# Position transform of the Fourier branch: plain fp32 products in place of split ones

## The chip, the core and the metric

The kernel runs on one core of a Trainium2 chip. Its engines work side by side, each on its own queue: TensorE (PE in the profile; its weight loads are a row of their own, PEld) multiplies matrices, VectorE (DVE) and ScalarE (ACT) work on elements, GpSimd (POOL) does little here, and SyncE's queue (SP) issues the DMAs. The metric is the time of one execution on the device in microseconds (us), the median of several runs. Before the change it is 1631.18 us (3 runs, 1630.85 to 1631.53).

## What is computed

Two layers of an encoder on 256 positions with 1024 channels. Each has a mixer of three branches (window attention, a state-space scan, a Fourier mixing) behind one input projection, then a cross-attention into 256 memory tokens, then a gated feed-forward. The change touches the Fourier branch only: six groups of 256 channels, of each the real part of the two-dimensional DFT over positions and channels.

```python
f = f_in.reshape(bsz, seq, FOURIER_GROUPS, FOURIER_GROUP_DIM).astype(f32)
f = jnp.fft.fft2(f, axes=(1, 3), norm="ortho").real.astype(h.dtype).reshape(bsz, seq, FOURIER_WIDTH)
y_fourier = f @ w_b_fourier
```

## The kernel before

**Split products.** Large products are made of three products in a reduced fp32 format (F32R): a value is split into a high part, its F32R rounding, and a low part, the rest. `mm3` (lines 352 to 355) adds high x high, high x low and low x high in PSUM. The weights come as a stream of 1 MB pieces on SP's queue (`load_next`, L313); each piece is split by an ACT cast (L323) and a DVE subtraction (L324) into `wh` and `wl`, up to three pieces ahead. `lin` (products with 512 columns, lines 353 to 355) and `lina` (256 columns, lines 414 to 416) run the projections over them. Attention and scan use plain fp32 products (`T.matmul` on fp32 tiles: L603, L648, L848, L849).

**The Fourier branch.** The input projection is taken in the order of `ORDER`; its first three tokens in each layer are f0, f1 and f2, and then bc, k0, x0 and the rest. One f token gives 512 columns, two channel groups. `lin` yields them for the positions 0 to 127 (`tt` = 0) and 128 to 255 (`tt` = 1). `f_done` folds the two halves, since cosine and sine over 256 positions are symmetric: sum and difference of the halves. It copies the first half out of PSUM on ACT (L1086), adds and subtracts on DVE (L1088, L1089), and splits both results, each with an ACT cast (L1091) and a DVE subtraction (L1092).

`fourier_chunk` then runs in two stages. The first is the position transform: for each group `j`, half `ct` of its channels and parity `e`, a product of 128 channels (stationary) with a 128x128 table of cosines and sines (moving, 128 columns) into `pg`, by `mm3`. Then ACT copies one half (L919), DVE forms sums and differences `uv` (L920, L921), ACT and DVE split them (L923, L924). The second stage is the channel transform with 264 and 256 columns, again by `mm3`, then the evacuation (L942 to L952). The table `c_dft` has six 128x128 blocks: two for the first stage, four for the second. `dft_parts` loads it in each layer (L895) and splits all six (L897, L898).

**What sets the order.** `lin` and `lina` write the main sequence. Other work is written as generators in four lanes (`n`, `s`, `a`, `f`); Fourier work is in lane `f`. After each half piece `pump` adds credit and lets the lanes take steps, and a step charges what it yields (`yield 0.9`). `yield 3, 0` means that the step wants three free 4 KB slots and no 2 KB slot; `slot` forces steps when slots become few. `yield LATER` holds the lane back for some pumps. A scheduler at compile time then orders the instructions of each engine; inside `ordered()` TensorE's own order is kept as written. On the chip each queue runs in order.

Of the kernel before, what the change touches and what calls it, by code (L numbers as in the profile page):

```python
# [11 lines left out]
F32 = mybir.dt.float32  # L12
F32R = mybir.dt.float32r
# [4 lines left out]
P = 128  # L18
# [153 lines left out]
def trunk(ctx: ExitStack, tc: tile.TileContext, a, out):  # L172
    nc = tc.nc
    V, A, T, G = nc.vector, nc.scalar, nc.tensor, nc.gpsimd
# [19 lines left out]
    def slot(size, shape, dt):  # L194
        keep = 0 if running[0] else RESERVE
        while len(slots[size]) <= keep and step():
            pass
        if not slots[size]:
            raise RuntimeError(f"no slot of {size} KB")
        r = slots[size].popleft()  # L200
        t = r.tile(shape, dt, name=nm("s%d_" % size))
        owner[id(t)] = (size, r, t)
        return t

    def s4(shape, dt=F32):
        return slot(4, shape, dt)

    def s2(shape, dt=F32):
        return slot(2, shape, dt)

    def free(*ts):
        for t in ts:
            if isinstance(t, (tuple, list)):
                free(*t)
            else:
                size, r, _ = owner.pop(id(t))
                slots[size].append(r)
# [25 lines left out]
    def bg(gen, lane="s"):  # L243
        lanes[lane].append(gen)
# [103 lines left out]
    def ordered():  # L348

        return tc.manual_schedule(engines={mybir.EngineType.PE})  # L350

    def mm3(o, sh, sl, mh, ml, start, stop):
        T.matmul(o, sh, mh, start=start, stop=False)  # L353
        T.matmul(o, sh, ml, start=False, stop=False)  # L354
        T.matmul(o, sl, mh, start=False, stop=stop)  # L355
# [66 lines left out]
    def fl(tiles):  # L422
        return lambda kt: tiles[kt // 4]
# [54 lines left out]
    def norms(n):  # L478

        drain_until(lambda: len(lanes["n"]) <= n, "n")  # L480
# [14 lines left out]
    def ftiles(n):  # L495
        return [(s4([P, 4, S], F32R), s4([P, 4, S], F32R)) for _ in range(n)]
# [263 lines left out]
    def bc_fin(bc, idx):  # L760

        def fin(v):
            hi, lo = bc
            A.copy(hi[:, idx:idx + 2, :], v)
            V.tensor_sub(lo[:, idx:idx + 2, :], v, hi[:, idx:idx + 2, :].bitcast(F32))
            yield 0.6
        return fin
# [122 lines left out]


    def dft_parts(R):
        yield 3, 0
        r = s4([P, 6, P])
        nc.sync.dma_start(r, a["c_dft"])  # L895
        hi, lo = R["dft"] = s4([P, 6, P], F32R), s4([P, 6, P], F32R)
        A.copy(hi, r)  # L897
        V.tensor_sub(lo, r, hi.bitcast(F32))  # L898
        free(r)
        yield 0.9  # L900

    def fourier_chunk(l, c, f, FT, R):


        yield 2, 0

        Gt = (s4([P, 2, 2, S], F32R), s4([P, 2, 2, S], F32R))
        dh, dl = R["dft"]
        for j in range(2):
            yield 0, 2  # L910
            pg = tp().rearrange("p (a b) -> p a b", a=2)
            with ordered():
                for ct in range(2):
                    cs = slice((2 * j + ct) * P, (2 * j + ct + 1) * P)
                    for e in range(2):
                        mm3(pg[:, ct, e * P:e * P + P], f[0][:, e, cs], f[1][:, e, cs], dh[:, e, :], dl[:, e, :],
                            True, True)
            t0, uv = s2([P, S]), s2([P, 2, S])
            A.copy(t0, pg[:, 0, :])  # L919
            V.tensor_add(uv[:, 0, :], t0, pg[:, 1, :])  # L920
            V.tensor_sub(uv[:, 1, :], t0, pg[:, 1, :])  # L921
            hi, lo = (t[:, :, j, :] for t in Gt)
            A.copy(hi, uv)  # L923
            V.tensor_sub(lo, uv, hi.bitcast(F32))  # L924
            free(t0, uv)
            yield 1.3
        free(f)
        yield LATER
        yield 2, 0
        out_ = FT[c] = (s4([P, 4, S], F32R), s4([P, 4, S], F32R))  # L930
        gp = [t.rearrange("p u j (b k) -> p u (j b) k", b=2) for t in Gt]
        for cp_ in range(2):

            qc, qs = (t[:, :4 * n].rearrange("p (j k) -> p j k", j=4) for t, n in ((tp(), 66), (tp(), 64)))
            with ordered():
                for m, o, k0, k1 in ((2, qc, 0, 66), (4, qs, 64, 128)):
                    m += cp_
                    mm3(o, dh[:, m, :], dl[:, m, :], gp[0][:, cp_, :, k0:k1], gp[1][:, cp_, :, k0:k1], True, True)
            yield 0, 2
            pc = s2([P, 4, 66])  # L940
            fo = s2([P, 2, S])
            A.copy(pc, qc)  # L942
            p4 = pc.rearrange("p (j b) k -> p j b k", j=2)
            q4 = qs.rearrange("p (j b) k -> p j b k", j=2)

            V.tensor_sub(fo[:, :, 0:P].rearrange("p j (m b) -> p j b m", b=2), p4[:, :, :, 0:64], q4)
            V.tensor_add(fo[:, :, P + 2:S:2], p4[:, :, 0, 63:0:-1], q4[:, :, 0, 63:0:-1])
            V.tensor_add(fo[:, :, P + 1:S:2], p4[:, :, 1, 63::-1], q4[:, :, 1, ::-1])
            A.copy(fo[:, :, 0:S:P], p4[:, :, 0, 0:65:64])
            hi, lo = (t.rearrange("p (j e) k -> p j e k", e=2)[:, :, cp_, :] for t in out_)  # L950
            A.copy(hi, fo)
            V.tensor_sub(lo, fo, hi.bitcast(F32))  # L952
            free(pc, fo)
            yield 1.8
        free(Gt)
        if R.get("f") == 2:
            free(R["dft"])
        R["f"] = R.get("f", 0) + 1
# [30 lines left out]
    for l in range(L):  # L989
# [10 lines left out]
        def to_T(kind, g):  # L1000
            t = s4([P, 2, 512])
            qkv[kind, g] = t

            def f(tt, ch, ps):
                A.copy(t[:, tt, :], ps)
            return f

        R = {}
# [58 lines left out]
        def xbc_pieces(blk, fin_of):  # L1067
            def f(n0, ps):
                pair = (n0 - X0) // 256 - blk // 2
                bg(conv_pair(ps, blk + 2 * pair, cw, fin_of(pair)))  # L1070
            lina(hb, 2, f)
# [3 lines left out]
        for n, tok in enumerate(ORDER):  # L1075
            k, g = tok[0], int(tok[1]) if tok[1].isdigit() else 0
            sg = [2] if n == 0 else None
            if k == "f":
                ft = (s4([P, 2, 512], F32R), s4([P, 2, 512], F32R))

                fs = []

                def f_done(tt, ch, ps, ft=ft, fs=fs):
                    if tt == 0:
                        fs.extend((s2([P, 512]), s2([P, 512])))
                        A.copy(fs[0], ps)  # L1086
                        return
                    V.tensor_add(fs[1], fs[0], ps)  # L1088
                    V.tensor_sub(fs[0], fs[0], ps)  # L1089
                    for e, t in enumerate(fs[::-1]):  # L1090
                        A.copy(ft[0][:, e, :], t)  # L1091
                        V.tensor_sub(ft[1][:, e, :], t, ft[0][:, e, :].bitcast(F32))  # L1092
                    free(fs)

                lin(hb, 2, f_done, seg=sg, mid=sg and (lambda: norms(0)))
                bg(fourier_chunk(l, g, ft, FT, R), "f")
            elif tok == "bc":
                dt_columns()
                Bt, Ct = ftiles(2)
                xbc_pieces(16, lambda pr: bc_fin(Bt, 2 * pr))  # L1100
                xbc_pieces(20, lambda pr: bc_fin(Ct, 2 * pr))
                bg(cb_task(l, Bt, Ct, R))
            elif k == "x":
                xT = s4([P, 2, 512])
                xbc_pieces(4 * g, lambda pr: x_fin([xT], pr))
                bg(ssd_group(l, g, xT, R, Dbc, ys))
            elif k in "qkv":
                lin(hb, 2, to_T(k, g), seg=sg, par=True)
                if k == "v":
                    bg(attn_group(l, g, qkv["q", g], qkv["k", g], qkv["v", g], gq[:, 2:3], R), "a")  # L1110
            elif k == "z":
                zt = s4([P, 2, 512])
                lin(hb, 2, lambda tt, ch, ps, zt=zt: A.activation(zt[:, tt, :], ps, AF.Silu))
                bg(ssd_gate(l, g, zt, ys, yT))
            elif k == "G":
                ga = gates(g)
            elif tok == "BF":
                drain_until(lambda: R.get("f") == 3, "f")
                branch(fl(FT), 8, ga)
                free(*FT.values(), ga)  # L1120
            elif tok == "BA":
                drain_until(lambda: "oT" in R and R.get("a"), "a")
                branch(fl(R["oT"]), 2, ga)
                free(R["oT"], ga)
# [304 lines left out]
```

## Time and profile before

| | |
|---|---|
| median of 3 runs | 1631.18 us (1630.85 to 1631.53) |
| profiled execution | 1631.55 us, its span 1629.8 us |
| TensorE busy | 1611.2 us, 99% of the span, 10354 products |
| DVE busy | 1164.7 us, 71% |
| ACT busy | 974.2 us, 60% |
| POOL busy | 45.9 us, 3% |
| granted TensorE clock | full, in all 40 slices |
| weights and data from HBM | 293.65 MB, 181 GB/s over the span |
| chain that ended last | PE 94%, ACT 3%, DVE 2%, issue 1% |

The span is the time between the first and the last instruction of the profiled execution; the 1.75 us beyond it lie around it. A product's end in the trace is modelled and overlaps the next product, so a busy TensorE row is not TensorE at its peak: the distance from one start to the next tells what a product costs in the queue. A wait is put down to the event that came last.

### The profile page before, as it was taken

The page shows a single profiled execution, that of the slowest core. Times are in us where ns is not written, and L with a number is a line of the kernel's source. Part 1 is how long each engine was busy: PE and PEld are TensorE (multiplying, and loading weights), DVE is VectorE, ACT ScalarE, POOL GpSimd, SP SyncE. Part 2 cuts the span into 40 slices and gives each one's busy share as a digit, 9 for nine tenths or more (in the row PEclk, how much of TensorE's full clock was granted, in tenths as well). Part 3 has the DMA queues.
Part 4 walks back from the last instruction along what each step waited for, and adds up shares of the span by engine and source line. Part 5 has one row for each costly group of instructions (what it writes and reads, how often), then busy time and mean ns, then how long its engine had stood idle before and what let it go on. Part 6 is the DMA issues. An engine that isn't in the chain of part 4 may idle for free.

```text
span 1629.8 us, 25584 instructions
## 1 busy us (share of the span) xinstructions
PE 1611.2 (99%) x10354; PEld 1454.3 (89%) x10354; DVE 1164.7 (71%) x1803; ACT 974.2 (60%) x1639; POOL 45.9 (3%) x47
## 2 busy tenths in 40 slices
PE   7999999999999999999999999999999999999998
PEld 6899988898998888999879998888989988889997
DVE  6898878788966665555479988868888676665543
ACT  6566667778745665444355667677786357554441
POOL 0000000000100100000000000000000001000000
PEclk9999999999999999999999999999999999999999
DMA  8445754656556544555553567555455555445552
GB/s 280 152 153 188 237 202 149 203 172 178 194 177 228 178 156 156 206 181 192 181 170 123 175 213 226 195 170 180 168 187 194 182 206 181 143 158 179 183 189 93
DMA packets 84302, 296.52 MB, mean 182 GB/s; under 512 B 7529, under 2 KB 46825, under 8 KB 53976
## 3 DMA queue, kind: packets, MB, share of 16 engines
q1 hardware_dynamic: 84184, 294.89, 54.0%
q8 instruction: 81, 1.33, 0.3%
q14 instruction: 37, 0.30, 0.1%
HBM read 293.65 MB, written 1.22 MB: 181 GB/s over the span
## 4 chain that ended last, share of the span: by engine, by line
PE 94%; ACT 3%; DVE 2%; issue 1%; POOL 0%; DMA 0%; SPq 0%; DVEq 0%; ACTq 0%; POOLq 0%
PE acc L354 14%; PE acc L355 14%; PE acc L353 14%; PE acc L415 13%; PE acc L414 13%; PE acc L416 13%; PE tp L848 2%; ACT wh L323 2%; PE tp L353 1%; PE tp L355 1%; PE tp L354 1%; PE tp L849 1%; PE tp L473 1%; PE tp L648 1%; PE tp L603 1%; DVE wl L324 1%
## 5 line engine op out<-in xcount | busy, mean ns | idle before, releaser
L324 DVE TENSOR_TENSOR wl<-wr,wh 128x2048 fp32r<-128x2048 f32 (+2 forms) x260 | 573.3, 2207 | 283.9 <-ACT wh L323 283.3
L323 ACT CAST wh<-wr 128x2048 fp32r<-128x2048 f32 (+2 forms) x260 | 477.4, 1839 | 402.2 <-issue 181.2
L414 PE MATMUL acc<-s,wh 128*128 128x256 f32 x1856 | 527.9, 285 | 0.0
L415 PE MATMUL acc<-s,wh 128*128 128x256 f32 x1856 | 526.6, 284 | 0.0
L416 PE MATMUL acc<-s,wl 128*128 128x256 f32 x1856 | 525.5, 283 | 0.0
L353 PE MATMUL acc<-wh,s 128*128 128x512 f32 x1072 | 427.7, 399 | 0.0
L354 PE MATMUL acc<-wl,s 128*128 128x512 f32 x1072 | 424.4, 396 | 0.4 <-DVE wl L324 0.4
L355 PE MATMUL acc<-wh,s 128*128 128x512 f32 x1072 | 423.7, 396 | 0.0
L415 PEld LDWEIGHTS acc<-s,wh 128*128 128x128 f32 x1856 | 356.1, 192 | 1.3 <-issue 0.5
L414 PEld LDWEIGHTS acc<-s,wh 128*128 128x128 f32 x1856 | 355.8, 192 | 1.6 <-issue 0.9
L416 PEld LDWEIGHTS acc<-s,wl 128*128 128x128 f32 x1856 | 355.8, 192 | 0.0
L355 PEld LDWEIGHTS acc<-wh,s 128*128 128x128 f32 x1072 | 203.6, 190 | 41.6 <-issue 1.4
L353 PEld LDWEIGHTS acc<-wh,s 128*128 128x128 f32 x1072 | 203.9, 190 | 41.2 <-issue 1.9
L354 PEld LDWEIGHTS acc<-wl,s 128*128 128x128 f32 x1072 | 203.8, 190 | 41.0 <-issue 0.9
L689 DVE SCALAR_TENSOR_TENSOR s<-s,cw,s 128x253 f32<-128x253 f32 (+2 forms) x288 | 121.7, 476 | 1.1 <-ACT s L686 0.7
L820 ACT ACTIVATE s<-s,nacs 128x128 f32<-128x128 f32 x128 | 44.6, 394 | 15.2 <-DMA s<-dd 13.9
L823 ACT ACTIVATE s<-s,dt 128x128 f32<-128x128 f32 x128 | 43.8, 395 | 2.7 <-DVE s L604 2.1
L821 DVE SCALAR_TENSOR_TENSOR s<-s,nacs,s 128x128 f32<-128x128 f32 x128 | 41.5, 344 | 5.0 <-ACT s L820 5.0
L353 PE MATMUL tp<-s,s 128*128 128x256 f32 (+2 forms) x152 | 42.8, 284 | 1.7 <-ACT s L923 1.5
L355 PE MATMUL tp<-s,s 128*128 128x256 f32 (+2 forms) x152 | 42.6, 283 | 0.5 <-DVE s L1092 0.5
L354 PE MATMUL tp<-s,s 128*128 128x256 f32 (+2 forms) x152 | 42.4, 280 | 0.0
L489 DVE TENSOR_TENSOR s<-tp,s 128x512 fp32r<-128x512 f32 x56 | 36.6, 683 | 5.6 <-ACT s L488 5.6
(223 smaller groups left out, 1419.7 us busy)
## 6 DMA issues: line engine op xcount, KB each, us to landing
wr<-in_wstream SPq DMA_DIRECT2D x236, 1024.0 KB, 4.9
s<-dd SPq DMA_DIRECT2D x32, 512.0 KB, 5.3
wr<-in_wstream SPq DMA_DIRECT2D x16, 768.0 KB, 4.4
s<-vd SPq DMA_DIRECT2D x12, 256.0 KB, 6.1
wr<-in_wstream SPq DMA_DIRECT2D x8, 256.0 KB, 4.7
s<-in_ssd_norm_g SPq DMA_DIRECT2D x8, 256.0 KB, 5.4
s<-in_memT SPq DMA_DIRECT2D x4, 512.0 KB, 5.9
X<-in_x SPq DMA_DIRECT2D x2, 512.0 KB, 3.8
```

The costliest lines, as they stand in the source:

```text
L323: A.copy(hi[:, c], raw[:, c])
L324: V.tensor_sub(lo[:, c], raw[:, c], hi[:, c].bitcast(F32))
L353: T.matmul(o, sh, mh, start=start, stop=False)
L354: T.matmul(o, sh, ml, start=False, stop=False)
L355: T.matmul(o, sl, mh, start=False, stop=stop)
L414: T.matmul(o, hi[:, w0:w0 + P], sh[:, k, :], start=kt == 0, stop=False)
L415: T.matmul(o, hi[:, w0:w0 + P], sl[:, k, :], start=False, stop=False)
L416: T.matmul(o, lo[:, w0:w0 + P], sh[:, k, :], start=False, stop=kt == npk - 1)
L689: V.scalar_tensor_tensor(v[:, b, i0:i1], u[:, b, i0 + k - 3:i1 + k - 3], c[:, k:k + 1], v[:, b, i0:i1], op0=ALU.mult, op1=ALU.add)
L820: A.activation(E[:, j, :], b[:, 1, :], AF.Identity, bias=nacs[:, tt, 32 + hf:33 + hf])
L821: V.scalar_tensor_tensor(E[:, j, :], b[:, 0, :], nacs[:, tt, hf:hf + 1], E[:, j, :], op0=ALU.add, op1=ALU.min)
L823: A.activation(W[:, j, :], cbd[:, tt, 0, :], AF.Copy, scale=dt[:, tt, hf:hf + 1])
```

## The change

`dft_parts` loads the two blocks of the first stage into a plain fp32 tile `dt_` (a 2 KB slot) and the four of the second into a scratch tile; only these four are split, into the two halves of one 4 KB tile `hl`. `f_done` writes sum and difference into one plain fp32 tile of the chunk and no longer splits them; the copy of the first half goes into the same tile. The first stage of `fourier_chunk` multiplies the two plain tiles with one fp32 product in place of `mm3`. The second stage reads the same four blocks from `hl`. The credit charged for the constants is 0.7 in place of 0.9, and the step wants two 4 KB slots and one 2 KB slot in place of three 4 KB slots.

```diff
--- before.py
+++ after.py
@@ -890,14 +890,17 @@
 
 
     def dft_parts(R):
-        yield 3, 0
-        r = s4([P, 6, P])
-        nc.sync.dma_start(r, a["c_dft"])
-        hi, lo = R["dft"] = s4([P, 6, P], F32R), s4([P, 6, P], F32R)
-        A.copy(hi, r)
-        V.tensor_sub(lo, r, hi.bitcast(F32))
+        yield 2, 1
+
+        dt_, r = s2([P, 2, P]), s4([P, 4, P])
+        nc.sync.dma_start(dt_, a["c_dft"][:, 0:2])
+        nc.sync.dma_start(r, a["c_dft"][:, 2:6])
+        hl = s4([P, 2, 4, P], F32R)
+        A.copy(hl[:, 0], r)
+        V.tensor_sub(hl[:, 1], r, hl[:, 0].bitcast(F32))
         free(r)
-        yield 0.9
+        R["dft"] = dt_, hl
+        yield 0.7
 
     def fourier_chunk(l, c, f, FT, R):
 
@@ -905,7 +908,7 @@
         yield 2, 0
 
         Gt = (s4([P, 2, 2, S], F32R), s4([P, 2, 2, S], F32R))
-        dh, dl = R["dft"]
+        dt_, hl = R["dft"]
         for j in range(2):
             yield 0, 2
             pg = tp().rearrange("p (a b) -> p a b", a=2)
@@ -913,8 +916,7 @@
                 for ct in range(2):
                     cs = slice((2 * j + ct) * P, (2 * j + ct + 1) * P)
                     for e in range(2):
-                        mm3(pg[:, ct, e * P:e * P + P], f[0][:, e, cs], f[1][:, e, cs], dh[:, e, :], dl[:, e, :],
-                            True, True)
+                        T.matmul(pg[:, ct, e * P:e * P + P], f[:, e, cs], dt_[:, e, :], start=True, stop=True)
             t0, uv = s2([P, S]), s2([P, 2, S])
             A.copy(t0, pg[:, 0, :])
             V.tensor_add(uv[:, 0, :], t0, pg[:, 1, :])
@@ -933,9 +935,9 @@
 
             qc, qs = (t[:, :4 * n].rearrange("p (j k) -> p j k", j=4) for t, n in ((tp(), 66), (tp(), 64)))
             with ordered():
-                for m, o, k0, k1 in ((2, qc, 0, 66), (4, qs, 64, 128)):
+                for m, o, k0, k1 in ((0, qc, 0, 66), (2, qs, 64, 128)):
                     m += cp_
-                    mm3(o, dh[:, m, :], dl[:, m, :], gp[0][:, cp_, :, k0:k1], gp[1][:, cp_, :, k0:k1], True, True)
+                    mm3(o, hl[:, 0, m, :], hl[:, 1, m, :], gp[0][:, cp_, :, k0:k1], gp[1][:, cp_, :, k0:k1], True, True)
             yield 0, 2
             pc = s2([P, 4, 66])
             fo = s2([P, 2, S])
@@ -1076,21 +1078,15 @@
             k, g = tok[0], int(tok[1]) if tok[1].isdigit() else 0
             sg = [2] if n == 0 else None
             if k == "f":
-                ft = (s4([P, 2, 512], F32R), s4([P, 2, 512], F32R))
-
-                fs = []
-
-                def f_done(tt, ch, ps, ft=ft, fs=fs):
+                ft = s4([P, 2, 512])
+
+                def f_done(tt, ch, ps, ft=ft):
+                    u, v = ft[:, 0, :], ft[:, 1, :]
                     if tt == 0:
-                        fs.extend((s2([P, 512]), s2([P, 512])))
-                        A.copy(fs[0], ps)
+                        A.copy(v, ps)
                         return
-                    V.tensor_add(fs[1], fs[0], ps)
-                    V.tensor_sub(fs[0], fs[0], ps)
-                    for e, t in enumerate(fs[::-1]):
-                        A.copy(ft[0][:, e, :], t)
-                        V.tensor_sub(ft[1][:, e, :], t, ft[0][:, e, :].bitcast(F32))
-                    free(fs)
+                    V.tensor_add(u, v, ps)
+                    V.tensor_sub(v, v, ps)
 
                 lin(hb, 2, f_done, seg=sg, mid=sg and (lambda: norms(0)))
                 bg(fourier_chunk(l, g, ft, FT, R), "f")
```

## Rows read from the trace of the kernel before

**Rows 1.** The page: busy time, share of the span and instructions, two engines

```profile
PE 1611.2 (99%) x10354; PEld 1454.3 (89%) x10354; DVE 1164.7 (71%) x1803; ACT 974.2 (60%) x1639; POOL 45.9 (3%) x47
```

**Rows 2.** Stretches: length, PE, PEld, DVE, ACT, POOL busy, clock, DMA share, GB/s

```profile
60.00:120.00 60.00, 59.90 (x455) 57.47 (x454) 59.36 (x114) 36.85 (x60) 0.00 (x0) 1.00 0.47 155
...
880.00:940.00 60.00, 60.00 (x458) 57.84 (x457) 59.68 (x110) 38.61 (x57) 0.00 (x0) 1.00 0.48 160
```

**Rows 3.** Groups by shape on TensorE: count | busy us, mean ns | idle before

```profile
L648 PE MATMUL tp<-s,s 128*128 128x128 f32 x128 | 16.7, 276 | 0.0
...
L353 PE MATMUL tp<-s,s 128*128 128x128 f32 x48 | 12.8, 273 | 0.2 <-ACT s L942 0.2
```

**Rows 4.** TensorE in order of time (start, duration, us), first stage: first and last of 22

```profile
48.04 0.27 PE L355 MATMUL tp<-s,s 128*128 128x128 f32 x1
...
50.38 0.28 PE L355 MATMUL tp<-s,s 128*128 128x128 f32 x1
```

**Rows 5.** TensorE in order of time: eight plain records among split products, two places

```profile
354.45 0.28 PE L415 MATMUL acc<-s,wh 128*128 128x256 f32 x1
...
354.81 0.28 PE L415 MATMUL acc<-s,wh 128*128 128x256 f32 x1
354.93 1.16 PE L648 MATMUL tp<-s,s 128*128 128x128 f32 x8
...
356.05 0.28 PE L414 MATMUL acc<-s,wh 128*128 128x256 f32 x1
...
400.98 0.39 PE L353 MATMUL acc<-wh,s 128*128 128x512 f32 x1
...
401.44 0.40 PE L355 MATMUL acc<-wh,s 128*128 128x512 f32 x1
401.68 1.05 PE L648 MATMUL tp<-s,s 128*128 128x128 f32 x8
...
402.80 0.39 PE L354 MATMUL acc<-wl,s 128*128 128x512 f32 x1
```

**Rows 6.** Groups by shape on ACT and DVE: count | busy us, mean ns | idle

```profile
L1091 ACT CAST s<-s 128x512 fp32r<-128x512 f32 x12 | 7.0, 616 | 4.1 <-DVE s L1088 4.0
...
L1092 DVE TENSOR_TENSOR s<-s,s 128x512 fp32r<-128x512 f32 x12 | 7.9, 686 | 0.0
...
L898 DVE TENSOR_TENSOR s<-s,s 128x768 fp32r<-128x768 f32 x2 | 1.9, 954 | 0.3 <-ACT s L897 0.3
```

**Rows 7.** Waits of TensorE's weight loads: us in total, times, longest us

```profile
PEld tp L355 <- DVE s L1092: 2.0, 4, 0.7
PEld tp L353 <- ACT s L923: 1.9, 1, 1.9
...
PEld acc L354 <- DVE wl L324: 0.8, 1, 0.8
...
PEld tp L353 <- ACT s L1091: 0.6, 2, 0.4
```

**Rows 8.** The chain that ended last, in order of time: start us, us, what

```profile
42.64 1.20 DVE s L1092 x2
...
45.81 0.52 PE tp L353 x2
...
59.05 1.04 ACT s L1091 x2
...
853.11 1.30 DVE s L1092 x2
```

**Rows 9.** ACT in order of time, first f piece of layer 0

```profile
26.65 1.35 ACT L1091 CAST s<-s 128x512 fp32r<-128x512 f32 x2 [3.77 <-DVE s L1088]
```

**Rows 10.** SP's queue in order of time; DMA issues: KB each, median us to landing

```profile
25.61 0.43 SPq L895 DMA_DIRECT2D s<-in_c_dft  x1
...
s<-in_c_dft SPq DMA_DIRECT2D x2, 384.0 KB, 6.0
```

## The prediction

> **What bounds the kernel.** I read the profile's page first, for the busy shares. TensorE is busy for 1611.2 of the 1629.8 us of the span, DVE for 1164.7 [rows 1]. A busy TensorE row says little by itself, because a product's modelled end overlaps the next one, so the second view is the order of time on TensorE, and there the distance from one start to the next. In most stretches this distance is constant to a hundredth of a microsecond (0.12 us for a 256-column product, 0.23 us for a 512-column one [rows 5]), so TensorE is being fed without gaps and time taken off its queue comes off the end. The third view is the table of stretches: DVE is nearly full just behind the Fourier pieces of each layer, 59.36 of 60 us and 59.68 of 60 us [rows 2], while TensorE shows no idle time worth naming there. The fourth is the list of waits and the chain of work that ended last, which show where the Fourier work itself stops TensorE [rows 7, 8]. Only there do ACT and DVE operations of the changed lines stand on the path.
>
> **Products of the first Fourier stage (position transform).** Per chunk and `j` there are 2 `ct` x 2 `e` = 4 transforms, each three split products before, one plain fp32 product after. Two layers, three chunks and two `j` make 12 such groups, 48 transforms. The trace has them as three lines of 48 records with 128 columns [rows 3]. The mean duration of 273 ns is no price, since products overlap. The price is the distance of starts: 21 steps from 48.04 to 50.38 us, so 2.34 / 21 = 0.1114 us [rows 4]. A group of 12 takes 12 x 0.1114 = 1.34 us.
>
> What a plain fp32 product of this very shape costs is shown by the attention's product with the values (L648, 128x128 stationary, 128 columns). The code calls it 64 times and the trace has 128 records [rows 3], so one plain product is two records. Eight records, that is four products and exactly one group of the changed stage, stand between split products at two places. From 401.44 to 402.80 us there are 1.36 us for one 512-column product, the eight records and another 512-column product; less 2 x 0.23 us that leaves 0.90 us. From 354.81 to 356.05 us, between 256-column products, 1.24 - 2 x 0.12 = 1.00 us remain [rows 5]. These two include the cost of going over to plain products and back.
>
> So a group saves between 1.34 - 1.00 = 0.34 and 1.34 - 0.90 = 0.44 us, and 12 groups between 4.0 and 5.2 us. The changed groups stand among the 512-column products of the next Fourier piece, as the 0.90 us does, so I take 5.2 us. All of it lies on TensorE's queue, hence on the path.
>
> The Trainium skill speaks against this: "FP8 and Floating Point Precision", section "TensorE Precision Notes", says that true fp32 is four passes through the array, so a plain product would be one pass more than the three of the split form. Taken as four passes at the split product's price that would be a loss of 5.3 us; the trace has two records at about the pitch of one split product each, and the measured rows decide for the sum. (The rule gets its own rival below.)
>
> **Splitting of sums and differences.** Per Fourier piece `f_done` drops two ACT casts (L1091, 616 ns) and two DVE subtractions (L1092, 686 ns) [rows 6]: 12 x 0.616 = 7.4 us of ACT and 12 x 0.686 = 8.2 us of DVE in all. The sum and the difference on DVE stay; they write the chunk's tile directly, and ACT's copy of the first half goes into that tile as well. ACT and DVE are not the bound, so these 15.6 us as such are worth nothing. They count where TensorE waited behind them:
> - In layer 0 the chain that ended last runs through L1092 twice (1.20 us, at 42.64 us) into the wait that the second stage has at 45.81 us [rows 8]; the list puts 1.9 us of idle weight-load time to that wait (ACT L923) [rows 7].
> - In layer 1 TensorE's first-stage products wait for L1092 directly; the chain has 1.30 us of it at 853.11 us [rows 8], and the list has 2.0 us in four waits, and 0.6 us for the casts of L1091 [rows 7].
> - At 59.05 us the casts (1.04 us) stand in front of the evacuation that the dt columns' transposes wait for [rows 8].
> - At 26.65 us they stand, for 1.35 us, ahead of the cast of the next weight piece [rows 9]; its DVE half (L324) stops TensorE for 0.8 us soon after [rows 7].
>
> Together these waits are 2.0 + 1.9 + 0.8 + 0.6 = 5.3 us [rows 7]. They are counted on the weight loads; TensorE's products hide part of each behind the one still running, so 5.3 us is the upper bound and 0 the lower one. Of the largest, only the 1.2 us of L1092 is taken out of its chain, and TensorE will be there 0.4 to 0.8 us earlier because the group ahead of it is shorter, so what is late next is the same chain: first-stage sums on DVE, cast on ACT, second stage. I take 0.5 us there, 1.0 us for the waits on L1092 in layer 1, 0.5 us for the weight piece and 0.3 us for the transposes, in all 2.3 us.
>
> **Constants.** The 128x768 table is no longer split as a whole. 128x256 of it stay plain in a 2 KB slot; 128x512 are split as before. The DVE half was 954 ns for 768 columns and a 512-column subtraction takes 686 ns [rows 6], so some 0.3 us less per layer on DVE and about as much on ACT, off the path: I count nothing. One more DMA is issued on the SP queue behind the first; an issue takes 0.43 us [rows 10] and the weight loads queue behind it, whose pieces are three ahead: nothing, 0.9 us for both layers if that cover is gone. The first stage no longer waits for the split of the constants, only for their landing.
>
> **Slots and order.** A chunk's input holds one 4 KB slot instead of two, and no 2 KB slots for sums; the constants hold one 4 KB and one 2 KB slot instead of two of 4 KB. The credit charged for the constants falls from 0.9 to 0.7. With fewer DVE and ACT operations the compile-time order of the remaining ones may change. No row shows that; I bound it by the largest single wait of this stretch, 1.9 us [rows 7], in either direction, and take zero, since slots only become freer.
>
> **Sum.** 5.2 + 2.3 = 7.5 us off the profiled execution of 1631.55 us, which is 1624.05 us. That execution is 0.37 us above the median of the runs shown, so the forecast is 1624.0 us, 0.44% below the median.
>
> **The rivals.**
> - *Everything on the changed lines' path goes.* All 5.3 us of waits are recovered and the groups run at 0.90 us: 5.2 + 5.3 = 10.5 us, 1621 us. For it: removing operations shortens several chains at once. Against it: the second stage's chain is still there. Chance 0.12.
> - *A wait for the constants.* TensorE takes its queue in order. The table's DMA is issued at 25.61 us and lands 6.0 us later (median) [rows 10], at 31.6 us, while the first chunk's sums and, before, their splits were there by 26.65 + 1.35 = 28.0 us [rows 9]. If the plain products, no longer held back by the constants' split, are put in the queue at that place, TensorE stands up to 31.6 - 28.0 = 3.6 us in layer 0. That leaves 3.9 us of gain, 1627.7 us. Against it: the products need a place among some 50 ready ones of the next piece. Chance 0.12.
> - *DVE keeps the pace.* In the full stretch behind the Fourier pieces [rows 2] TensorE's lead is given back, because it arrives at split weights that DVE has not made yet; if DVE's relief falls into its own idle time before, the whole 7.5 us go and the time is 1631.5 us. Against it: DVE loses 6 x 0.686 + 0.3 = 4.4 us of work per layer ahead of that stretch, TensorE only 7.5 / 2 = 3.75 us. Chance 0.10.
> - *Slower: a plain product costs four times the split pitch.* Then a transform takes 4 x 0.1114 = 0.446 us instead of 0.334, so 48 x 0.111 = 5.3 us are added. The longer groups also delay the chain to the second stage, so that no wait is recovered: 1636.9 us. It decides as soon as eight records take over 1.34 us. Against it stand the 0.90 and 1.00 us of [rows 5]. This is what the four passes of the page "FP8 and Floating Point Precision" of the Trainium skill would make of it; the trace does not agree at 128 columns. Chance 0.05.
>
> **How the numbers follow.** The forecast itself has 0.61, between 1622.3 us (the range of the order's effect and of the waits) and 1627 us (the groups at 1.00 us and half of the waits). 0.2% of the time, about what a measurement of this kernel can tell from no change, is 3.3 us. Faster than that, below 1627.9 us, are the forecast, the first rival and half of the second: 0.61 + 0.12 + 0.06, less a little, 0.78. Within 0.2% are the other half of the second and the third: 0.16. Slower: 0.06, the fourth and a bad order. The range from 1621 to 1629 us holds the forecast and the first two rivals and leaves out the last two.
>
> **What would show it.** In the changed kernel the first stage should appear as 96 records of 128 columns with one line of its own, eight records in 0.90 to 1.00 us with the return to split products. If they take over 1.34 us the fourth rival holds. Waits of TensorE on the two removed lines must be gone, and the wait of the second stage on ACT's cast should be under 1.9 us. A wait of the first plain product on the table's DMA near 31 us is the second rival. If the two layers' full DVE stretches end as late as before although the Fourier pieces ended earlier, it is the third. The prediction is wrong if the groups save what I say and a wait of several microseconds appears at another place in the Fourier stretch, which is the order's effect that I set at zero.

## The result: 0.57% faster, 9.6 us instead of the 7.5 us forecast

The changed kernel takes 1621.80 us (median of 4 runs, 1621.55 to 1623.84), the kernel before in the same comparisons 1631.36 us (4 runs, 1630.85 to 1632.65). The ratio is 0.9943, with a 95% interval of 0.9926 to 0.9960. That is 9.6 us less; the forecast of 1624.0 us is 2.2 us too high and the time lies inside the stated range. The profiled execution took 1621.86 us, its span 1620.1 us.

The page of the changed kernel (busy time, share, instructions), which answers to [rows 1]:

```profile
PE 1604.3 (99%) x10306; PEld 1449.6 (89%) x10306; DVE 1158.7 (72%) x1791; ACT 967.3 (60%) x1627; POOL 46.1 (3%) x47
```

There are 48 products fewer (144 split ones gone, 96 plain records come), and 12 operations fewer on DVE and on ACT. The stretches behind the Fourier pieces (length; PE, PEld, DVE, ACT, POOL busy; clock; DMA share; GB/s), beside [rows 2]:

```profile
60.00:120.00 60.00, 60.00 (x457) 57.84 (x457) 58.79 (x109) 38.53 (x62) 0.00 (x0) 1.00 0.48 160
880.00:940.00 60.00, 60.00 (x456) 57.84 (x456) 58.11 (x109) 39.41 (x67) 0.00 (x0) 1.00 0.49 162
```

DVE is still nearly full there, with 0.6 and 1.6 us less than before, and TensorE has no idle time at all.

The first stage is now one line, L919 (group by shape, beside the split line of [rows 3]):

```profile
L919 PE MATMUL tp<-s,s 128*128 128x128 f32 x96 | 12.3, 276 | 0.0
```

One group of eight records stands among 512-column products as the 0.90 us of [rows 5] did (TensorE in order of time, start and duration in us):

```profile
46.51 0.40 PE L355 MATMUL acc<-wh,s 128*128 128x512 f32 x1
46.74 1.05 PE L919 MATMUL tp<-s,s 128*128 128x128 f32 x8
47.55 0.48 PE L353 MATMUL acc<-wh,s 128*128 128x512 f32 x1
47.87 0.39 PE L354 MATMUL acc<-wl,s 128*128 128x512 f32 x1
```

From 46.51 to 47.87 us are 1.36 us; less two products of 0.23 us, 0.90 us remain. All 96 records, measured so in their runs of 4 to 16, take 10.99 us, 0.916 us a group. Before, 144 records at 0.1114 us took 16.04 us [rows 4]. The products' part is 5.05 us.

The waits of TensorE's weight loads on operations of the Fourier branch (us in total, times, longest) were the other part of the sum. All that is left of [rows 7] in the Fourier stretches of the changed kernel is this:

```profile
PEld tp L1063 <- ACT s L1060: 0.4, 2, 0.2
...
PEld tp L919 <- DVE s L1089: 0.2, 1, 0.2
PEld tp L919 <- DVE s L1088: 0.2, 1, 0.2
```

0.8 us, where the same sum was 6.5 us before: the 5.3 us of [rows 7] and three smaller rows of the same list,

```profile
PEld tp L1061 <- ACT s L1058: 0.6, 2, 0.3
...
PEld tp L353 <- ACT s L942: 0.4, 1, 0.4
...
PEld tp L354 <- DVE s L924: 0.2, 1, 0.2
```

So by subtraction the remaining 4.5 us of the gain lie in these waits. The order of time on TensorE agrees on the place. Counted from the first weight product of each trace, the 300th weight product (at 85 us before) comes 5.1 us earlier than before, the 4392nd (at 821 us) 4.3 us, the 4800th (at 912 us) and the last 9.3 us. Each layer's Fourier stretch gives about 5 us, and 0.8 us are given back between 390 and 520 us. Why the waits went, and so nearly all, was the question of the experiments.

### The profile page after: what moved, and what is told of

It is laid out like the page before. It is cut to its first block, busy times and chain, and to the rows that moved or that the text cites. A ratio compares the mean times of both kernels' runs of the same rounds, so it can differ in the third digit from the quotient of the medians.

```text
span 1620.1 us, 25470 instructions
## 1 busy us (share of the span) xinstructions
PE 1604.3 (99%) x10306; PEld 1449.6 (89%) x10306; DVE 1158.7 (72%) x1791; ACT 967.3 (60%) x1627; POOL 46.1 (3%) x47
## 4 chain that ended last, share of the span: by engine, by line
PE 95%; ACT 2%; DVE 1%; issue 1%; POOL 0%; DMA 0%; SPq 0%; DVEq 0%; POOLq 0%
PE acc L353 15%; PE acc L355 15%; PE acc L354 15%; PE acc L415 13%; PE acc L414 13%; PE acc L416 13%; PE tp L848 2%; PE tp L849 1%; PE tp L473 1%; ACT wh L323 1%; PE tp L353 1%; PE tp L355 1%; PE tp L354 1%; PE tp L603 1%; PE tp L648 1%; PE tp L919 1%
## 5 line engine op out<-in xcount | busy, mean ns | idle before, releaser
L353 PE MATMUL acc<-wh,s 128*128 128x512 f32 x1072 | 428.0, 399 | 0.0
L353 PEld LDWEIGHTS acc<-wh,s 128*128 128x128 f32 x1072 | 204.0, 190 | 41.2 <-issue 1.9
L689 DVE SCALAR_TENSOR_TENSOR s<-s,cw,s 128x254 f32<-128x254 f32 (+2 forms) x288 | 122.2, 476 | 1.2 <-ACT s L686 0.7
L824 DVE SCALAR_TENSOR_TENSOR s<-s,dt,s 128x128 f32<-128x128 f32 x128 | 40.0, 345 | 0.0
L1144 DVE TENSOR_TENSOR X<-X,acc 128x512 f32<-128x512 f32 x24 | 16.4, 683 | 26.2 <-PE acc L355 26.2
L457 ACT ACTIVATE s<-X 128x512 f32<-128x512 f32 x24 | 15.1, 629 | 33.4 <-DVE X L1144 30.9
```

The lines of the kernel that those rows point to most:

```text
L689: V.scalar_tensor_tensor(v[:, b, i0:i1], u[:, b, i0 + k - 3:i1 + k - 3], c[:, k:k + 1], v[:, b, i0:i1], op0=ALU.mult, op1=ALU.add)
```

## The experiments

Each of the runs below was compared with the kernel before on its chip (median 1631.8 to 1632.6 us there; 1631.36 us in the result above). One thing must be known to read the profiles: the first weight product starts between 10.6 and 12.4 us of the span, by when the first loads land. There is one profile of each kernel, so no run shows whether a late start belongs to the kernel or to the execution. A table at the end takes the start off.

### One part alone: plain products, splits kept

In the kernel before, the three products become one:

```diff
-    mm3(pg[...], f[0][:, e, cs], f[1][:, e, cs], dh[:, e, :], dl[:, e, :], True, True)
+    T.matmul(pg[...], f[ct][:, e, cs].bitcast(F32), dh[:, e, :].bitcast(F32), start=True, stop=True)
```

> The kernel before with one part of the change alone: one plain fp32 product per transform in the first stage, while sums and differences are still split by ACT and DVE and the constants and slots stay as before. The product reads the high parts for the first half of the channels and the low parts for the second, so it still waits for both splits; what is left out is the other part of each value and of the table. Theory (the gain is the sum of two separate parts): only the products' part is gained, 12 groups x (1.337 - 0.916) = 5.1 us, 1631.4 - 5.1 = 1626.3 us. Rival (the waits go because the shorter groups shift TensorE and DVE against each other): nearly all 9.5 us are gained, about 1622 us.

Measured: 1623.51 us, ratio 0.9952 (0.9938 to 0.9966), 8.3 us less by the medians. That is 3.2 us more than the products' part, and most of the way to the rival's 1622 us. My theory of two separate parts fell here. The waits of the weight loads in the Fourier stretch of layer 0 (20 to 90 us):

```profile
PEld acc L354 <- DVE wl L324: 0.8, 1, 0.8
PEld tp L353 <- ACT s L923: 0.3, 1, 0.3
```

and in that of layer 1 (815 to 900 us):

```profile
PEld tp L916 <- ACT s L1091: 0.7, 2, 0.4
...
PEld tp L916 <- DVE s L1092: 0.3, 1, 0.3
```

The 1.9 us ahead of the second stage (L353 on L923) have become 0.3 and the 2.0 us on L1092 half a microsecond over both layers, although every cast and subtraction of the split is still there. Only the 0.8 us for the weight piece and the 0.6 us on L1091 (0.7 here) stayed.

### The other part alone: sums unsplit, three products

```diff
-    ft = (s4([P, 2, 512], F32R), s4([P, 2, 512], F32R))
+    ft = s4([P, 2, 512], F32R)       # u, v written by the two sums, no casts, no subtractions
...
-    mm3(pg[...], f[0][:, e, cs], f[1][:, e, cs], dh[:, e, :], dl[:, e, :], True, True)
+    mm3(pg[...], f[:, e, cs], f[:, e, cs], dh[:, e, :], dl[:, e, :], True, True)
```

> The kernel before with the other part alone: sum and difference are written unsplit into one F32R tile, without the ACT casts and DVE subtractions, and each transform is still three F32R products (the low part's place is taken by the same tile, so the low part of the sums is left out). Theory: only the waits are gained, 9.5 - 5.1 = 4.4 us, 1627.0 us; the waits of TensorE on the two removed lines and the one on the cast ahead of the second stage in layer 0 are gone, the 144 products cost what they did. The sum of my prediction had 2.3 us for this: 1629.1 us. Rival (DVE and ACT are no bound, their relief is worth nothing by itself): 1631.4 us.

Measured: 1631.81 us, ratio 0.9996 (0.9987 to 1.0005). The relief of 15 us of ACT and DVE work alone gave nothing that the medians show; between 2.1 us less and 0.8 us more is possible. The waits on L1091 and L1092 are gone, of course, but in layer 1 the first stage now waits for the sums themselves (L1087 0.9 us, L1086 0.2 us), and the largest wait is not gone (layer 0, 20 to 90 us):

```profile
PEld tp L353 <- ACT s L923: 2.3, 1, 2.3
```

### Where the largest wait came from

The order of DVE's queue at the first chunk of layer 0 shows it (start, duration in us). Before:

```profile
39.68 2.29 DVE L324 TENSOR_TENSOR wl<-wr,wh 128x2048 fp32r<-128x2048 f32 x1 [0.46 <-ACT wh L323]
41.89 0.41 DVE L920 TENSOR_TENSOR s<-s,tp 128x256 f32<-128x256 f32 x1
...
42.55 1.29 DVE L1092 TENSOR_TENSOR s<-s,s 128x512 fp32r<-128x512 f32 x2
43.76 0.69 DVE L924 TENSOR_TENSOR s<-s,s 128x512 fp32r<-128x512 f32 x1
```

With plain products alone:

```profile
38.87 0.42 DVE L920 TENSOR_TENSOR s<-s,tp 128x256 f32<-128x256 f32 x1 [0.95 <-ACT s L919]
...
41.77 2.29 DVE L324 TENSOR_TENSOR wl<-wr,wh 128x2048 fp32r<-128x2048 f32 x1 [0.66 <-ACT wh L323]
43.98 1.28 DVE L924 TENSOR_TENSOR s<-s,s 128x512 fp32r<-128x512 f32 x2
```

Before, the first-stage sums (L920) stand behind a 2.29 us weight subtraction, and the chain of [rows 8] runs from there into the second stage. With plain products alone the compile-time order puts them ahead of it. TensorE's order differs too. The number of 512-column products between the last first-stage product and the first second-stage product of that chunk, beside the list's wait ahead of the second stage, is

| kernel | products between | wait on the cast, us |
|---|---|---|
| sums unsplit only | 10 | 2.3 |
| before | 12 | 1.9 |
| two split products (below) | 14 | 0.7 |
| plain products only | 16 | 0.3 |
| before, held by one pump in layer 0 (below) | 18 | 0.6 |
| constants as before (below) | 22 | 0.3 |
| changed | 23 | none |
| split as idle work (below) | 25 | none |

The wait falls with that number, though not strictly. In the changed kernel the weight subtraction is ahead of the sums again (their first one, L922, starts at 41.61 us), but 23 products cover the chain (TensorE in order of time):

```profile
39.27 0.48 PE L354 MATMUL acc<-wl,s 128*128 128x512 f32 x1
...
44.58 0.41 PE L353 MATMUL tp<-s,s 128*128 128x264 f32 x2
```

The 5.3 us between them cover what stands between the stages. But the chain itself is shorter too: before it took 3.9 us, from the first-stage sums at 41.89 us to the second stage at 45.81 us [rows 8], and now the last cast ends at 43.66 us, 2.05 us after the first sum (ACT):

```profile
42.38 1.28 ACT L925 CAST s<-s 128x512 fp32r<-128x512 f32 x2 [2.47 <-DVE s L923]
```

The 1.29 us of L1092 that stood in it are gone. An estimate of the shares from these numbers: with 12 products instead of 23 the second stage would have come 11 x 0.23 = 2.5 us earlier, at 42.1 us, and waited 1.6 us; with 23 products and the 1.29 us back it would have waited 0.4 us. By this estimate the place carries most of the 1.9 us, and the removed subtractions the rest.

### Constants as before

Against the changed kernel, in short:

```diff
-    dt_, hl = R["dft"]      # two blocks plain, four split, credit 0.7
+    dh, dl = R["dft"]       # all six split, credit 0.9; the products read dh
```

> The changed kernel with the constants as before: all six blocks of the table loaded by one DMA, split by one cast and one subtraction into two 4 KB slots, credit 0.9 and three slots wanted; the plain products read the table's high part (its low part is left out). Theory: constants, slots and credit are worth nothing, 1621.8 us within 0.7 us. Rival (the freed slot, the order or the shorter split of the constants carries the 2 us that the forecast missed): 1623.5 us or more.

Measured: 1622.34 us, ratio 0.9943 (0.9931 to 0.9956), the same ratio as the changed kernel's. Constants, their slot and their credit are worth nothing that shows. The interval still holds the rival's least value, 1623.5 us; the profiled execution, 0.1 us from the changed kernel's behind the start, speaks against it.

### Plain products doubled

```diff
-    T.matmul(pg[...], f[:, e, cs], dt_[:, e, :], start=True, stop=True)
+    for k in range(2):
+        T.matmul(pg[...], f[:, e, cs], dt_[:, e, :], start=k == 0, stop=k == 1)
```

> The changed kernel with each plain product of the first stage run twice into the same place (its result is doubled): 48 plain products more, nothing else. It measures the price of one plain product on the path. Theory: two records of 0.1117 us each, 48 x 0.2234 = 10.7 us more than the changed kernel, 1632.5 us, a little less where a wait covers them. Rival (four passes at the split pitch): 48 x 0.446 = 21.4 us more, 1643.2 us. If TensorE were not the bound there: 1622 us.

Measured: 1632.24 us, 10.4 us above the changed kernel, 0.217 us for each of the 48 products; in the profiled executions, behind their first weight product, it is 9.3 us, 0.19 us each. Its trace has two groups in one run of 32 records:

```profile
38.52 0.39 PE L353 MATMUL acc<-wh,s 128*128 128x512 f32 x1
38.75 3.73 PE L920 MATMUL tp<-s,s 128*128 128x128 f32 x32
42.23 0.48 PE L354 MATMUL acc<-wl,s 128*128 128x512 f32 x1
42.55 0.40 PE L355 MATMUL acc<-wh,s 128*128 128x512 f32 x1
```

4.03 us less 0.46 us are 3.57 us, 0.223 us for each of 16 products, and 21.4 us for four passes at the split pitch are refuted. TensorE is the bound in the Fourier stretch: what its queue gains or loses there arrives at the end almost in full, 9.3 to 10.4 of the 10.7 us.

### Holding the second stage back

Three kernels hold the lane back twice ahead of the second stage of every chunk:

```diff
     yield LATER
+    yield LATER
     yield 2, 0
```

> The kernel before with one line more: the second Fourier stage of each chunk is held back twice in its lane (a second hold ahead of its constants' use), so that on TensorE it stands 42 products of the next piece behind the first stage of layer 0 instead of 12. Products and splits are those of before. Theory (the waits are a matter of the place at which the second stage stands in TensorE's queue): the wait of 1.9 us on ACT's cast ahead of the second stage is gone and part of the waits on the splits in layer 1 with it, about 2 to 3 us gained, 1628.8 us. Rival (the waits go only if the ACT and DVE operations of the split go): no gain, 1631.7 us.

> The kernel with unsplit sums and three products (second experiment) with the second stage held back twice as well. The low part of the sums is left out as there. Theory (place in the queue and unsplit sums together make the waits): 24 products instead of 10 stand between the first stage and the second in layer 0, the wait of 2.3 us on ACT's cast that remained there is gone, and the whole 4.4 us of waits are gained: 1627.2 us. Rival (only shorter products free the waits): 1631.7 us.

> The changed kernel with the second stage held back twice. In it TensorE no longer waits in the Fourier stretch, so there is nothing to gain: 1621.8 us within 0.7 us. Rival (a later second stage costs or gains by itself, and the two runs with the hold measure that): more than 1 us away.

Measured: 1675.88, 1674.44 and 1665.95 us, ratios 1.0270 (1.0249 to 1.0291), 1.0261 (1.0240 to 1.0283) and 1.0206 (1.0189 to 1.0224). The edit was too coarse to decide: the wait ahead of the second stage is gone from all three, as the theory wants, but the later chunks' second stages land inside attention and scan and the times are 34 to 43 us above the kernel before. Not all of that is waiting: TensorE's granted clock is 0.990, 0.987 and 0.993 in the mean of the three profiled executions, which by itself can make up to 17, 22 and 12 us (estimates: the share of the clock that is missing, times the span). The longest waits of TensorE in the changed kernel with the hold:

```profile
PE tp L638 <- ACT s L616: 10.5, 4, 5.0
...
PE tp L774 <- ACT s L578: 6.5, 2, 3.2
PE tp L648 <- ACT s L639: 2.8, 2, 1.4
```

Two finer ones hold the first chunk only, by two pumps in both layers and by one pump in layer 0 (five lines that handle the hold shift the line numbers by up to 7):

```diff
     yield LATER
+    if not c:            # the other: if not c and not l
+        yield "p2"       # the other: "p1"
     yield 2, 0
```

> The kernel before with the second stage of the first chunk of each layer held back by two pumps more, a finer hold than in the three held kernels. Products and splits are those of before. In TensorE's order 30 products instead of 12 now stand between the first chunk's stages in layer 0, and 44 instead of 20 in layer 1; later chunks move by at most 48 products and no further work is displaced. Theory (the waits ahead of the second stage, and of the next chunk's first stage behind it, are a matter of the place in the queue): about 3 us gained, 1628.8 us, the wait on ACT's cast ahead of the second stage gone from the list. Rival (they go only with the split operations or with shorter products): 1631.7 us.

> The kernel before with the second stage of the first chunk of layer 0 alone held back by one pump more: 18 products instead of 12 stand ahead of it, 1.4 us more cover; layer 1 keeps its order. Theory: of the 1.7 us that TensorE stands there 1.4 us are gained, 1630.3 us. Rival: 1631.7 us.

Measured: 1643.48 us, ratio 1.0066 (1.0053 to 1.0078), and 1635.39 us, ratio 1.0015 (1.0006 to 1.0024); neither the theories' gain nor the rivals' standstill. The wait on the cast is gone in the first, and others stand in its place (waits of TensorE's products, whole span, behind the wait for the first loads):

```profile
PE acc L421 <- DVE wl L329: 2.8, 2, 1.4
...
PE tp L1068 <- ACT s L1065: 2.4, 2, 1.4
PE tp L853 <- DVE s L836: 1.9, 4, 1.0
PE tp L358 <- ACT s L949: 0.8, 1, 0.8
```

The Fourier work that comes later meets DVE in its full stretch (this kernel, columns as above):

```profile
60.00:120.00 60.00, 58.96 (x445) 56.38 (x444) 58.34 (x110) 37.86 (x61) 0.00 (x0) 1.00 0.43 147
```

TensorE loses 1.0 us there, where it lost 0.1 us [rows 2]. That is the smaller part: of the 10 us that this kernel has over the one before, behind the start, 0.4 us arise in each Fourier stretch and the rest in the stretches behind them, where the clock was also at the lower of its two levels for two times 3.4 us.

The second, one pump in layer 0, is the cleanest test of the place. With 18 products instead of 12 the wait on the cast fell from 1.9 to 0.6 us (20 to 90 us), and TensorE stood 0.5 instead of 1.5 us between 40 and 50 us, with every cast and subtraction in place. The gain was lost again behind it:

```profile
PEld tp L358 <- DVE s L955: 1.5, 2, 1.1
...
PEld tp L358 <- ACT s L928: 0.6, 1, 0.6
PEld tp L359 <- DVE s L929: 0.5, 1, 0.5
```

TensorE stood 1.0 us for the evacuation's subtraction (L955), up to 77.66 us, and then its clock was at the lower level, 1.2 GHz, until 84.6 us (columns as above):

```profile
74.00:88.00 14.00, 13.01 (x84) 12.66 (x83) 11.46 (x26) 7.90 (x19) 0.00 (x0) 0.76 0.31 106
```

A mean of 0.76 over 14 us is 3.4 us lost. That and 0.7 us more of waits are the 4.1 us that this profiled execution has over the kernel before, behind the start; the two of its runs with a granted clock of 1.000 took 1632.06 and 1633.41 us, within the range of the kernel before (1630.98 to 1633.45 us). Before, TensorE stood 1.5 us near 44 us and its clock stayed full. So the place of the second stage does decide its own wait, but moving it alone, in the kernel before, moves the wait to other places, and what was lost beyond that is in good part the clock.

### Second stage plain as well

```diff
-    mm3(o, hl[:, 0, m, :], hl[:, 1, m, :], gp[0][:, cp_, :, k0:k1], gp[1][:, cp_, :, k0:k1], True, True)
+    T.matmul(o, r[:, m, :], gp[:, cp_, :, k0:k1], start=True, stop=True)
```

> The changed kernel with the second stage in plain fp32 products too (264 and 256 columns), its splits on ACT and DVE left out and its constants no longer split. By the trace a plain record of 256 columns has a distance of 0.217 us (L603, four records in 0.867 us), a split product of 256 to 264 columns 0.119 to 0.123 us. Theory (a plain product is two records whose moving side costs two array passes each, so it is cheaper only where the weight load sets the pace): 24 products x (0.433 - 0.365) = 1.6 us more, 1623.4 us, since no wait is left that the missing splits could shorten. Rival (the price per product holds at any width): 24 x 0.14 = 3.4 us less, 1618.4 us.

Measured: 1622.25 us, ratio 0.9938 (0.9924 to 0.9952): no difference to the changed kernel that can be seen, and between the theory's 1623.4 us and the rival's 1618.4 us. The price per product is the theory's:

```profile
61.79 0.28 PE L416 MATMUL acc<-s,wl 128*128 128x256 f32 x1
61.91 1.92 PE L933 MATMUL tp<-s,s 128*128 128x264 f32 x8
63.48 0.47 PE L414 MATMUL acc<-s,wh 128*128 128x256 f32 x1
63.78 0.28 PE L415 MATMUL acc<-s,wh 128*128 128x256 f32 x1
```

1.99 us less two products of 0.12 us are 1.75 us for eight records, 0.219 us each; the twelve split products took 1.48 us in the changed kernel. At 256 and 264 columns a plain product is the dearer one, by 6 x 0.27 = 1.6 us in all. The count of weight products, as in the result above, shows where this came back: the two Fourier stretches take 0.5 and 0.6 us more than in the changed kernel, and the stretch between them 1.3 us less. This kernel has 14 operations fewer on ACT and as many on DVE; which of them made that is open.

### Two split products, and the split as idle work

```diff
-    mm3(pg[...], f[0][:, e, cs], f[1][:, e, cs], dh[:, e, :], dl[:, e, :], True, True)
+    T.matmul(o, f[0][:, e, cs], dh[:, e, :], start=True, stop=False)
+    T.matmul(o, f[1][:, e, cs], dh[:, e, :], start=False, stop=True)
```

> The kernel before with two F32R products per transform instead of three (low x high table is kept, high x low table is left out); splits, constants and slots are those of before. Two such products take 2 x 0.1114 = 0.223 us, which is what one plain product takes (0.223 us in the changed kernel). Theory (what counts is how long the first stage holds TensorE, and with it the place of its sums in DVE's queue): as with plain products alone, 48 x 0.1114 = 5.3 us plus about 3 us of waits, 1623.5 us; the first chunk's sums stand ahead of the weight subtraction in DVE's queue as there. Rival (the waits go only where the product is plain): 1631.9 - 5.3 = 1626.6 us.

Measured: 1626.46 us, ratio 0.9965 (0.9953 to 0.9978). The products' 5.3 us came, the waits did not go; the time is the rival's 1626.6 us. The sums do stand ahead of the weight subtraction as I expected, but in layer 1 the first stage waits for the split as before (815 to 900 us):

```profile
PEld tp L918 <- DVE s L1093: 1.2, 4, 0.5
PEld tp L917 <- ACT s L1092: 0.9, 2, 0.5
```

and a new one of 1.3 us appears at the dt columns in layer 0. So the same time on TensorE, by another kind of product, gave another order and other waits. It is not the length of the first stage alone. One difference of the two edits was not tested apart: with plain products alone only the second half of a group reads the low parts, here every second product does, so the subtraction is needed earlier; part of the difference on L1092 can come from that.

The last run puts the split back into the changed kernel as work that nobody reads:

```diff
     V.tensor_sub(v, v, ps)
+    hi, lo = s4([P, 2, 512], F32R), s4([P, 2, 512], F32R)
+    for e, t in enumerate((u, v)):
+        A.copy(hi[:, e, :], t)
+        V.tensor_sub(lo[:, e, :], t, hi[:, e, :].bitcast(F32))
+    free(hi, lo)
```

> The changed kernel with the removed split put back as idle work: two casts on ACT and two subtractions on DVE per piece into two 4 KB tiles that nobody reads. It parts the last 1.5 us, which the changed kernel has over plain products alone. Theory (the split costs by taking time on ACT and DVE ahead of weight pieces and evacuations): about 1623.4 us. Rival (it costs because the first stage waits for its results): 1621.9 us, no change.

Measured: 1623.96 us, ratio 0.9947 (0.9934 to 0.9961). By the median that is the theory's 1623.4 us, but the ratio lies close to the changed kernel's 0.9943 and the profiled execution started 1.4 us later, so it is inconclusive. The 0.8 us wait for the weight piece is back in its list.

### The runs on one table

For each profiled execution: the span less the start of the first weight product; the difference to before; and what would follow from two numbers alone, the first stage's time on TensorE (products' part) and the sum of the weight-load waits on ACT and DVE in the two Fourier stretches (without those of the norms, L465 and L488).

| kernel | span - start, us | to before | products' part | waits, us | both together |
|---|---|---|---|---|---|
| before | 1629.8 - 10.8 | | | 6.5 | |
| changed | 1620.1 - 10.6 | -9.5 | -5.05 | 0.8 | -10.8 |
| plain products only | 1621.7 - 10.8 | -8.1 | -5.05 | 2.9 | -8.7 |
| sums unsplit only | 1628.9 - 12.1 | -2.2 | 0 | 3.8 | -2.7 |
| two split products | 1625.5 - 12.3 | -5.8 | -5.3 | 5.9 | -5.9 |
| constants as before | 1620.4 - 10.8 | -9.4 | -5.05 | 1.4 | -10.2 |
| split as idle work | 1622.2 - 12.0 | -8.8 | -5.05 | 1.9 | -9.7 |
| products doubled | 1631.2 - 12.4 | -0.2 | +5.4 | 0.8 | -0.3 |
| second stage plain | 1620.3 - 11.0 | -9.7 | -3.4 | 0.8 | -9.1 |

The last column agrees with the third within 1.3 us. It is mostly the larger in size: the changed kernel gives back 0.8 us outside the two stretches, and a wait of the weight load can be covered by the product still running; the second stage in plain products is the exception. The third column agrees with the medians within 0.8 us but for the unsplit sums, which have 2.2 us less here and nothing by the medians. Two terms account for the change; the second one is in the main not a price of the split, but of where things stand.

## Why the prediction was right, and where it was off

- **What bounds the kernel: right.** What was put into TensorE's queue in the Fourier stretch came out at the end (0.19 to 0.217 us for each of 48 products run twice), and so did what was taken out.
- **The products' term: right.** 5.2 us forecast from the 0.90 us of [rows 5], 5.05 us measured. The rival of four times the split pitch is out: eight records took 0.90 to 1.04 us. The Trainium skill's four passes ("FP8 and Floating Point Precision", section "TensorE Precision Notes") come near the rows at 256 and 264 columns: two records of 0.219 us are 3.6 times a split product's 0.123 us. At 128 columns the trace does not agree: two records of 0.11 us are twice a split product's 0.11 us, and the measurement decides.
- **The waits' term: the step that was mis-sized.** I took 2.3 us out of an upper bound of 5.3 us; 4.5 us came. The bound had left out the smaller rows, 1.2 us. For the largest wait the prediction said that the same chain would be late next and gave it 0.5 us. That took the order of the queues as fixed. In the changed kernel 23 instead of 12 products stand ahead of the second stage, and the wait is gone altogether. It is for the most part the order's effect, which I had set at zero in the step on slots and order, with 1.9 us as its bound. The range held the result because its lower end was the first rival's time; the forecast's own band began at 1622.3 us, above the 1621.8 us measured, and that the time came out so near is in part luck. (The other end of that band, 1627 us, does not follow from its terms: 1631.55 - 4.0 - 1.15 = 1626.4 us.)
- **The reason for the waits' term: half wrong.** I credited them to the removed casts and subtractions. Removed alone, these gave nothing by the medians and at most about 2 us; plain products alone gave 3.2 us of waits, with all of the split in place. The 0.8 us for the weight piece are the split's, as I said: they stayed with plain products alone, came back with the idle split, and are absent from every kernel without the split.
- **Constants: right.** Nothing that a run of their own shows.
- **The rivals.** The first (all waits go, 1621 us) is what nearly came. There was no wait for the table: its two DMAs are issued at 29.99 and 30.98 us, later than before, and the first product stands at 37.56 us. DVE's full stretch did not take the lead back: it is 5.1 us at 85 us and the same at 302 us.

What stays open: why the compile-time order falls one way with plain products and another with two split ones of the same length. No run took that apart; the five holds moved the second stage, but each moved other work too, and in all of them the clock fell for a part of the time.

## What to carry to other kernels

Price a plain fp32 product by the distance of starts at its own width: at 128 columns it is two records at the pitch of one split product each, 0.22 us against 0.33 us for three split ones; at 256 to 264 columns it is 0.44 against 0.37 us. Take waits as a separate term, and bound it by the whole of the list, since an edit to one stage lets the scheduler reorder the queues around it. Freed time on engines that are not the bound was worth little here, nothing by the medians, until the order changed too. And look at the granted clock of each stretch before a longer time is put down to waits: a hold that took 1.3 us off one wait cost 3.4 us by the clock.

## What was not expected of the hardware

- The start of an execution differs: the first weight product began between 10.6 and 12.4 us of the span, with the same loads: the load of `in_c_oh`, on which the chain stands first, took 4.76 us before and 6.32 us with the products doubled. Differences of a microsecond between single profiles have to be read behind that point.
- In the changed kernel with the long hold TensorE's granted clock fell in a stretch where it stood for long (length; PE, PEld, DVE, ACT, POOL busy; clock):

```profile
400.00:440.00 40.00, 31.44 (x203) 26.94 (x202) 32.83 (x73) 25.17 (x50) 0.70 (x1) 0.87 0.38 128
```

TensorE was busy for 31.4 of the 40 us and had 0.87 of its clock in the mean, so part of that time it ran at the lower of its two levels; in the changed kernel the same stretch has 40.0 us and the full clock. Waits there cost more than their own length.
